# Weights of a seven-product matrix stage prepared three products ahead, with two weight sums in places of their own and one low part on VectorE

## The chip, the cores and the metric

One core of one Trainium2 chip runs the whole program. The metric is the device time of one execution in microseconds (us), the median of several runs. TensorE multiplies, VectorE, ScalarE and GpSimd (POOL) work on tiles in the on-chip memory, and SyncE (SP) issues most of the transfers. Each engine takes its instructions in the order of its own queue and waits on semaphores for the others, so an instruction that waits holds up all behind it on that engine.

## What is computed

One layer of a hybrid decoder trunk in float32: three token mixers (causal pooling, RWKV-7, attention into 256 memory tokens), merged by gates, then a convolutional feed-forward part. The change lies in the feed-forward part, which is, for 1024 tokens of width 1024 and an inner width of 2816:

```python
h = rms_norm(x, norm_ffn_pre[l])
u = causal_dwconv(h @ w_ffn_up[l], conv_w[l], conv_b[l])      # 3 taps along the tokens
u_gate, u_val = jnp.split(u, 2, axis=-1)
f = (jax.nn.gelu(u_gate, approximate=True) * u_val) @ w_ffn_down[l]
x = x + rms_norm(f, norm_ffn_post[l])
```

## The kernel before

**Blocks and pairs.** The inner width is 22 blocks of 128 (NF). A pair i is gate block i and value block 22 + i of `w_ffn_up`. Blocks 0 to 4 are made earlier in another way, in halves of 512 tokens; pairs 5 (EARLY) to 21, 17 in all, run through `up_pair` (L998 to L1079), called by the loop at L1323. The down product `f @ w_ffn_down` follows as passes over 128-wide steps (`down_pass`, `step`).

**Seven products.** The up product of a pair is a 2 × 2 block product: two weight blocks, two halves of the width 1024 (4 slices of 128 each), two halves of the tokens (512 each). It is done with seven products instead of eight, on sums of the quarters. With a11 and a12 the two halves of the gate block, and a21 and a22 those of the value block, the weights of products 0 to 6 are

0: a11; 1: s1 = a21 + a22; 2: s2 = s1 − a11; 3: a12; 4: a11 − a21; 5: a12 − s2; 6: a22.

The token side (panels B11, T1, T2, B21, T3, B22, T4) is made once, ahead of the stage. The results are put together again as they come.

**Float32 out of parts.** Each weight and each panel is kept as a high part, rounded to the matmul's format, and a low part, the rest. `mm3` (L168 to L170) does three matmuls per slice: high × high, high × low, low × high. A product is 4 slices × 3 = 12 matmuls of 128 × 128 by 512 columns, a pair 84, the stage 17 × 84 = 1428.

**What a pair does on each engine.**

- SP loads four weight quarters of two 128 KB pieces each (L1008; `a` in the trace), into places that alternate by the parity of the pair, and stores the result `d_f[i]` (L1079).
- `parts` (L1014): for each of the seven weights ScalarE casts the high part (L1027) and POOL subtracts it from the source for the low part (L1028), in two instructions each, one per 256 columns. The results lie in one of six `wt` places used in turn. So the weights of product m can be written when product m − 6 is through on TensorE.
- `both` (L1010 to L1013): the weight sums, two instructions each. s1 and s2 on POOL, in one tile `sm`, s2 over s1; a11 − a21 over a21 and a12 − s2 over `sm` on VectorE.
- The sums of results: ScalarE copies products 0 and 1 out of PSUM (L1057, L1059), VectorE adds the others (L1061 to L1076; those named `psf` read PSUM).
- The convolution: ScalarE starts it (L1044, 1024 columns, for each block), VectorE adds two taps (L1046, four instructions a pair). ScalarE's gelu (`act`, L200), VectorE's product of gate and value (L1078), the store.

**What sets the order.** `up_pair` writes the steps in the order of the products. A scheduler then orders each engine's queue by what is ready, so parts of the next pair come between those of the pair that is being finished. `last_low` and `last_sum` keep the last POOL low part and the last L1072, behind which the first steps of the down stage are ordered (`later`).

**After the stage.** In the last pair, `down_loads` issues the first three rows of the down product, `X[k]` (rows of `d_f`, L1301), and weights `fw` (L1312), on SP's queue. `step` casts weight and row on ScalarE (L1355) and makes the low parts (L1359) on VectorE or POOL; the results of the down matmuls are `psd`.

The code of the stage, with the line numbers of the profile:

Of the kernel before, what the change touches and what calls it, by code (L numbers as in the profile page):

```python
# [9 lines left out]
F32 = mybir.dt.float32  # L10
FR = mybir.dt.float32r
AF = mybir.ActivationFunctionType
ALU = mybir.AluOpType
# [4 lines left out]
P = 128  # L18
T = 1024
# [9 lines left out]
NF = 22  # L29
# [15 lines left out]
def trunk_kernel(ctx: ExitStack, tc: tile.TileContext, xT, memT, pvec, w_in, w_kv, w_upd, w_upg,  # L45
                 w_pool, w_ppool, w_pmem, w_prwkv, w_o, w_fup, w_fdn, out):
    nc = tc.nc
    V, A, G, PE, SP = nc.vector, nc.scalar, nc.gpsimd, nc.tensor, nc.sync

    const = ctx.enter_context(tc.tile_pool(name="const", bufs=1))  # L50
    wp = ctx.enter_context(tc.tile_pool(name="wp", bufs=1))
    psg = ctx.enter_context(tc.tile_pool(name="psg", bufs=2, space=PSUM))
    psk = ctx.enter_context(tc.tile_pool(name="psk", bufs=1, space=PSUM))
    pss = ctx.enter_context(tc.tile_pool(name="pss", bufs=2, space=PSUM))
# [13 lines left out]
    d_f = dtile([NF, P, T], "d_f")  # L68
# [5 lines left out]
    def col(name, i):  # L74
        o, w = PV[name]
        return pv[:, o + i:o + i + 1]
# [18 lines left out]
    for lo in (0, 64):  # L95
        s = slice(lo, lo + 64)
# [3 lines left out]
    for lo in (0, 64):  # L100
        s = slice(lo, lo + 64)
# [122 lines left out]
    for k in range(KC):  # L224
        tag = ("X01", "X11", "HV", "HV")[k // 2]
# [528 lines left out]
    with tc.tile_pool(name="km", bufs=1) as km:  # L754
# [240 lines left out]

    nwt, last_sum, last_low = [0], [None], [None]

    def up_pair(i):  # L998
        c = i % 2

        def load(nm, tag, j, k0):
            if i == EARLY:
# [3 lines left out]
            t = [wp.tile([P, 2, P], F32, name=nm, tag=f"{tag}{c}", bufs=4) for _ in range(2)]  # L1006
# [4 lines left out]
        def both(eng, out_, a, b, op):  # L1011
            for u in range(2):
                eng.tensor_tensor(out_[u], a[u], b[u], op=op)  # L1013

        def parts(src):

            n = nwt[0] % 6
            nwt[0] += 1
            if n < 2:
                w = ow.tile([P, 2, 4, P], FR, name="wt", tag=f"q{n}")  # L1020
                w = [w[:, 0], w[:, 1]]
            else:
                w = [pmp.tile([P, 4, P], FR, name=f"wt{e}", tag=f"n{8 + (n + 1) % 4 + 4 * e}")
                     for e in range(2)]
            for u in range(2):
                us = slice(2 * u, 2 * u + 2)
                A.copy(w[0][:, us], src[u])  # L1027
                last_low[0] = G.tensor_tensor(w[1][:, us], src[u], w[0][:, us].bitcast(F32), op=ALU.subtract).ins  # L1028
            return w

        nb = [0]

        def prod(src, panel):
            w = parts(src)
            pool, tag = ((psg, "g0"), (psg, "g1"), (pss, "s"), (psk, "k"), (psg, "g0"), (psg, "g1"),
                         (pss, "s"))[nb[0]]
            nb[0] += 1
# [3 lines left out]
            return ps  # L1041

        def convolved(z, d, j):
            A.activation(d, z, AF.Identity, scale=col("cw2", j), bias=col("cb", j))  # L1044
            for n, cw in ((1, "cw1"), (2, "cw0")):
                V.scalar_tensor_tensor(d[:, n:], z[:, :T - n], col(cw, j), d[:, n:], op0=ALU.mult,  # L1046
                                       op1=ALU.add)

        a11 = load("a11", "whi", i, 0)
        a21 = load("a21", "wlo", NF + i, 0)  # L1050
        a22 = load("a22", "wlo", NF + i, 4)
        a12 = load("a12", "whi", i, 4)
        sm = [wp.tile([P, 2, P], F32, name="sm", tag=f"wraw{c}", bufs=3) for _ in range(2)]
        z1, z2 = (ow1.tile([P, T], F32, name=f"z{e}", tag=f"q{4 + 2 * e + c}") for e in range(2))
        c11, c12, c21, c22 = z1[:, :512], z1[:, 512:], z2[:, :512], z2[:, 512:]
        u2 = ow.tile([P, 512], F32, name="u2", tag="xt", bufs=2)
        A.copy(c11, prod(a11, B11))  # L1057
        both(G, sm, a21, a22, ALU.add)
        A.copy(c22, prod(sm, T1))  # L1059
        both(G, sm, sm, a11, ALU.subtract)  # L1060
        V.tensor_tensor(u2, c11, prod(sm, T2), op=ALU.add)  # L1061
        V.tensor_tensor(c22, c22, u2, op=ALU.add)
        V.tensor_tensor(c11, c11, prod(a12, B21), op=ALU.add)
        both(V, a21, a11, a21, ALU.subtract)
        p7 = prod(a21, T3)
        third = V.tensor_tensor(c21, u2, p7, op=ALU.add).ins
        if i == NF - 1:
            down.extend(down_loads())
            down.append(third)
        both(V, sm, a12, sm, ALU.subtract)  # L1070
        V.tensor_tensor(c12, c22, prod(sm, B22), op=ALU.add)
        last_sum[0] = V.tensor_tensor(c22, c22, p7, op=ALU.add).ins  # L1072
        d1, d2 = (ow.tile([P, T], F32, name=f"d{e}", tag=f"q{2 + e}") for e in range(2))
        convolved(z1, d1, i)
        act(d1, d1, AF.Gelu_apprx_tanh)
        V.tensor_tensor(c21, c21, prod(a22, T4), op=ALU.add)  # L1076
        convolved(z2, d2, NF + i)
        V.tensor_tensor(d1, d1, d2, op=ALU.mult)  # L1078
        (G if i == NF - 1 else SP).dma_start(d_f[i], d1)  # L1079


    ow_ctx = ExitStack()
# [82 lines left out]
    EARLY = 5  # L1165
# [109 lines left out]
    class Sums:  # L1275
# [339 lines left out]
```

## Time and profile before

| what | us |
|---|---|
| median of 3 runs | 2079.53 (2077.59 to 2079.88) |
| the profiled execution | 2081.88, its span 2080.0 |
| TensorE busy | 2014.5 |
| VectorE, ScalarE, POOL busy | 1361.4, 1069.4, 812.5 |
| seven-product stage on TensorE | 339.8, from 1499.5 to 1839.3 |

The profiled execution lies 2.35 us above the median, and 1.88 us of it lie outside the span. In the views of the trace a row gives a group of instructions by source line, engine and operation as "output <- inputs"; `wt` are weights in parts, `a` the loaded quarters, `sm` the sums s1 and s2, `z` the results of the pair, `d` the convolved blocks, `psf` the PSUM tiles of the stage. "Idle before" is the time that the engine stood still before the instructions of a group, with what ended it. TensorE's busy time counts each matmul's record, and the record of a matmul that waits runs on, so the number of matmuls per window tells more than its busy share.

### The profile page before, as it was taken

How to read it: one execution, taken by the hardware profiler on the slowest of the kernel's cores; microseconds unless marked ns; L12 is line 12 of the kernel's file. 1: busy time of each engine (PE TensorE's matmuls, PEld its weight loads, DVE VectorE, ACT ScalarE, POOL GpSimd, SP SyncE). 2: the span in 40 equal slices, each digit the busy share in tenths (PEclk: the TensorE clock that was granted, in tenths of full speed). 3: DMA queues.
4: the chain of work that ended last, by engine and by line, in shares of the span. 5: the costliest groups of instructions: out<-in, count | busy, mean ns of one | idle time of the engine just before them, and what ended most of it. 6: DMA issues, size and time to landing. Idle time of an engine off the chain costs nothing.

```text
span 2080.0 us, 34125 instructions
## 1 busy us (share of the span) xinstructions
PE 2014.5 (97%) x12246; PEld 1558.7 (75%) x12246; DVE 1361.4 (65%) x2170; ACT 1069.4 (51%) x2249; POOL 812.5 (39%) x917
## 2 busy tenths in 40 slices
PE   8999999999999999999999999998999999989997
PEld 5777767776778667866878878876678777767886
DVE  6567437664667357823895443778777777767798
ACT  7585348623773367434566243546444443444644
POOL 5521213121222121212133355655588888832341
PEclk9999999999999999999999999999999999999999
DMA  4312211120212021214427343634322222169776
GB/s 155 130 41 74 67 59 61 65 82 22 87 61 98 24 89 61 78 51 133 160 82 234 123 142 110 213 123 135 109 72 76 79 74 83 64 189 261 166 181 149
DMA packets 176713, 221.83 MB, mean 107 GB/s; under 512 B 16544, under 2 KB 128288, under 8 KB 176544
## 3 DMA queue, kind: packets, MB, share of 16 engines
q1 hardware_dynamic: 163616, 204.44, 30.3%
q0 software_dynamic: 11856, 14.16, 4.2%
q8 instruction: 97, 1.59, 0.3%
q10 hardware_dynamic: 1072, 1.05, 0.2%
q14 instruction: 72, 0.59, 0.1%
HBM read 170.30 MB, written 49.28 MB: 106 GB/s over the span
## 4 chain that ended last, share of the span: by engine, by line
PE 30%; DVE 7%; DMA 5%; POOL 4%; issue 4%; ACT 3%; SPq 0%; POOLq 0%; ACTq 0%; DVEq 0%
PE psg L170 5%; PE psg L169 5%; PE psg L168 5%; POOL wt L1028 2%; PE psd L169 2%; PE psd L170 2%; PE psf L170 2%; PE psd L168 2%; PE psf L169 2%; PE psf L168 2%; POOL sm L1013 1%; DMA a<-in_w_fup 1%; DMA g<-d_zg 1%; DMA R<-d_f 1%; POOL wlo L132 1%
## 5 line engine op out<-in xcount | busy, mean ns | idle before, releaser
L132 POOL TENSOR_TENSOR wlo<-wraw,whi 128x256 fp32r<-128x256 f32 x472 | 411.6, 881 | 941.8 <-ACT whi L129 775.1
L168 PE MATMUL psg<-hh,whi 128*128 128x512 f32 x928 | 380.7, 410 | 2.7 <-DVE kv L315 2.7
L170 PE MATMUL psg<-hh,wlo 128*128 128x512 f32 x928 | 376.9, 406 | 0.2
L169 PE MATMUL psg<-hl,whi 128*128 128x512 f32 x928 | 375.8, 405 | 0.0
L129 ACT CAST whi<-wraw 128x256 fp32r<-128x256 f32 x472 | 182.7, 403 | 220.8 <-PE psg L169 108.0
L168 PEld LDWEIGHTS psg<-hh,whi 128*128 128x128 f32 x928 | 174.7, 188 | 43.3 <-DVE kv L315 4.0
L170 PEld LDWEIGHTS psg<-hh,wlo 128*128 128x128 f32 x928 | 174.5, 188 | 43.2 <-POOL wlo L132 5.3
L169 PEld LDWEIGHTS psg<-hl,whi 128*128 128x128 f32 x928 | 174.7, 188 | 39.5 <-issue 3.4
L1028 POOL TENSOR_TENSOR wt<-a,wt 128x256 fp32r<-128x256 f32 x136 | 133.8, 1013 | 31.3 <-ACT wt L1027 31.3
L168 PE MATMUL psd<-f,u 128*128 128x512 f32 x292 | 115.8, 397 | 8.2 <-ACT f L1355 4.8
L169 PE MATMUL psd<-f,u 128*128 128x512 f32 x292 | 115.6, 396 | 0.6 <-DVE f L1359 0.6
L170 PE MATMUL psd<-f,u 128*128 128x512 f32 x292 | 115.2, 396 | 0.0
L1028 POOL TENSOR_TENSOR wt<-sm,wt 128x256 fp32r<-128x256 f32 x102 | 106.8, 1066 | 19.2 <-ACT wt L1027 19.2
L170 PE MATMUL psf<-h2h,wt 128*128 128x512 f32 x272 | 108.8, 400 | 1.0 <-POOL wt L1028 0.6
L168 PE MATMUL psf<-h2h,wt 128*128 128x512 f32 x272 | 106.3, 391 | 1.7 <-ACT wt L1027 1.6
L169 PE MATMUL psf<-h2l,wt 128*128 128x512 f32 x272 | 106.0, 390 | 0.0
L1027 ACT CAST wt<-sm 128x256 fp32r<-128x256 f32 x102 | 37.9, 404 | 129.4 <-POOL sm L1013 124.1
L1046 DVE SCALAR_TENSOR_TENSOR d<-z,pv,d 128x1023 f32<-128x1023 f32 x68 | 91.6, 1347 | 12.0 <-ACT d L1044 9.5
L170 PE MATMUL psf<-t,wt 128*128 128x512 f32 x204 | 80.8, 396 | 3.4 <-POOL wt L1028 3.4
L686 DVE TENSOR_TENSOR HV<-ph,Hd 64x128 f32<-64x128 f32 x112 | 32.4, 289 | 72.2 <-PE ph L640 48.0
L168 PE MATMUL psf<-t,wt 128*128 128x512 f32 x204 | 79.6, 390 | 0.0
L169 PE MATMUL psf<-t,wt 128*128 128x512 f32 x204 | 79.5, 390 | 0.0
(424 smaller groups left out, 4750.7 us busy)
## 6 DMA issues: line engine op xcount, KB each, us to landing
wraw<-in_w_in SPq DMA_DIRECT2D x240, 128.0 KB, 2.4
a<-in_w_fup SPq DMA_DIRECT2D x128, 128.0 KB, 2.4
d_zg<-st SPq DMA_DIRECT2D x48, 256.0 KB, 2.7
wraw<-in_w_fup SPq DMA_DIRECT2D x80, 128.0 KB, 2.5
fw<-in_w_fdn SPq DMA_DIRECT2D x33, 256.0 KB, 4.2
fraw<-d_f SPq DMA_DIRECT2D x33, 256.0 KB, 5.3
wraw<-in_w_prwkv SPq DMA_DIRECT2D x64, 128.0 KB, 2.4
wraw<-in_w_o SPq DMA_DIRECT2D x64, 128.0 KB, 2.5
```

Of the source, the lines that this page charges most:

```text
L129: last_whi[0] = A.copy(hi, src).ins
L132: (V if lo_on_dve[0] else G).tensor_tensor(lo, src, hi.bitcast(F32), op=ALU.subtract)
L168: first = PE.matmul(ps, wh, xh, start=start, stop=False)
L169: PE.matmul(ps, wh, xl, start=False, stop=False)
L170: last_mm[0] = PE.matmul(ps, wl, xh, start=False, stop=stop).ins
L686: ready = V.tensor_tensor(HV[q, :, c + 1, e], ph[q], Hd[q], op=ALU.add).ins
L1013: eng.tensor_tensor(out_[u], a[u], b[u], op=op)
L1027: A.copy(w[0][:, us], src[u])
L1028: last_low[0] = G.tensor_tensor(w[1][:, us], src[u], w[0][:, us].bitcast(F32), op=ALU.subtract).ins
L1046: V.scalar_tensor_tensor(d[:, n:], z[:, :T - n], col(cw, j), d[:, n:], op0=ALU.mult, op1=ALU.add)
```

## The change

`up_pair` becomes a class `Pair` with a method for each part and a loop `up_pairs` that writes the steps in another order:

- **Three products ahead (AHEAD).** The weights of product m (cast, low part, the sums made for it) are written ahead of the matmuls and result sums of product m − 3. The six places of `wt` stay.
- **Loads and the first two sums one pair ahead.** `sums` issues a pair's four loads and makes s1 and s2 at the place where the pair before gets its weights of product 4. s1 has the places that `sm` had, s2 a place of its own (tag `ss`). Only in pair 5 s2 is still written over s1.
- **One low part on VectorE.** The low part of product 1 (weights s1) is made by VectorE instead of POOL: two instructions a pair, 34 in all.
- **Two orders.** s1 stands behind the last POOL low part written so far (`last_low`), a11 − a21 behind the last L1103 (`last_sum`).

What is computed, the matmuls and their order, and the order of the loads and stores on SP are the same.

```diff
-    def up_pair(i):
-        c = i % 2
+    def parts(src, eng):
...
-                last_low[0] = G.tensor_tensor(w[1][:, us], src[u], w[0][:, us].bitcast(F32), op=ALU.subtract).ins
+            low = eng.tensor_tensor(w[1][:, us], src[u], w[0][:, us].bitcast(F32), op=ALU.subtract)
+            if eng is G:
+                last_low[0] = low.ins
...
+    class Pair:
...
+        def weights(self, n):
+            if n == 2 and self.s2 is self.s1:
+                both(G, self.s2, self.s1, self.a11, ALU.subtract)
+            if n == 4:
+                both(V, self.a21, self.a11, self.a21, ALU.subtract, last_sum[0])
+            if n == 5:
+                both(V, self.s2, self.a12, self.s2, ALU.subtract)
+            src = (self.a11, self.s1, self.s2, self.a12, self.a21, self.s2, self.a22)[n]
+            return parts(src, V if n == 1 else G)
+
+        def sums(self):
+            self.a11 = self.load("a11", "whi", self.i, 0)
...
+            self.s1 = [wp.tile([P, 2, P], F32, name="s1", tag=f"wraw{self.c}", bufs=3) for _ in range(2)]
+            both(G, self.s1, self.a21, self.a22, ALU.add, last_low[0])
+            if self.i == EARLY:
+                self.s2 = self.s1
             else:
+                t = ow.tile([P, 4, P], F32, name="s2", tag="ss", bufs=2)
+                self.s2 = [t[:, :2], t[:, 2:]]
+                both(G, self.s2, self.s1, self.a11, ALU.subtract)
...
+    AHEAD = 3
+
+    def up_pairs(i0, i1):
+        pairs = [Pair(i) for i in range(i0, i1)]
+        pairs[0].sums()
+        steps = [(p, n) for p in pairs for n in range(7)]
+        ready = []
+        for m in range(len(steps) + AHEAD):
+            if m < len(steps):
+                p, n = steps[m]
+                if n == 4 and p is not pairs[-1]:
+                    pairs[p.i - i0 + 1].sums()
+                ready.append(p.weights(n))
+            if m >= AHEAD:
+                p, n = steps[m - AHEAD]
+                p.product(n, ready.pop(0))
...
-    for i in range(EARLY, NF):
-        up_pair(i)
+    up_pairs(EARLY, NF)
```

In the changed kernel the low part is L1011, the sums of weights L1018, the cast L1010, the convolution L1023 and L1025, the copies L1082 and L1085, the sums of results L1088 to L1110, the product L1112, the store L1113.

Three queues show the new order. In the rows below, a name's number is that of its tile; a pair's loads are four numbers apart each (first piece and second piece one apart), and from one pair to the next the numbers grow by some 180.

POOL before, in the middle of the stage. The weights are those of one pair, from product 0 (a_16302) to product 3 (a_16314), and a_16485 + a_16489 is s1 of the pair after it:

```order
L1028 TENSOR_TENSOR wt<-a_16302,wt 128x256
L1028 TENSOR_TENSOR wt<-a_16303,wt 128x256
L1013 TENSOR_TENSOR sm<-a_16485,a_16489 128x256
L1013 TENSOR_TENSOR sm<-a_16486,a_16490 128x256
L1028 TENSOR_TENSOR wt<-sm,wt 128x256 x2
L1013 TENSOR_TENSOR sm<-sm,a_16302 128x256
L1013 TENSOR_TENSOR sm<-sm,a_16303 128x256
L1028 TENSOR_TENSOR wt_16366<-sm,wt_16365 128x256 x2
L1028 TENSOR_TENSOR wt_16387<-a_16314,wt_16386 128x256
L1028 TENSOR_TENSOR wt_16387<-a_16315,wt_16386 128x256
```

The second sum (`sm<-sm,a_16302`) stands behind the low part of product 1 and ahead of that of product 2. POOL in the changed kernel, again from product 0 of a pair (a_16188) on:

```order
L1011 TENSOR_TENSOR wt<-a_16188,wt 128x256
L1011 TENSOR_TENSOR wt<-a_16189,wt 128x256
L1011 TENSOR_TENSOR wt_16322<-s_16208,wt_16321 128x256 x2
L1011 TENSOR_TENSOR wt_16347<-a_16200,wt_16346 128x256
L1011 TENSOR_TENSOR wt_16347<-a_16201,wt_16346 128x256
L1018 TENSOR_TENSOR s_16385<-a_16373,a_16377 128x256
L1018 TENSOR_TENSOR s_16386<-a_16374,a_16378 128x256
L1018 TENSOR_TENSOR s_16389<-s_16385,a_16369 128x256
L1018 TENSOR_TENSOR s_16389<-s_16386,a_16370 128x256
L1011 TENSOR_TENSOR wt_16395<-a_16192,wt_16394 128x256
L1011 TENSOR_TENSOR wt_16395<-a_16193,wt_16394 128x256
```

The low part of product 1 is gone from POOL, and both sums of the next pair (s_16385 and s_16389) stand behind the low part of product 3, ahead of that of product 4.

VectorE before, through the sums of results of one pair (z_17756, z_17757). a_17930 is a12 of the next pair, a_18102 a21 of the one after that:

```order
L1013 TENSOR_TENSOR a_18102<-a_18098,a_18102 128x256
L1013 TENSOR_TENSOR a_18103<-a_18099,a_18103 128x256
L1061 TENSOR_TENSOR u_17758<-z_17756,psf 128x512
L1062 TENSOR_TENSOR z_17757<-z_17757,u_17758 128x512
L1063 TENSOR_TENSOR z_17756<-z_17756,psf 128x512
L1013 TENSOR_TENSOR sm<-a_17930,sm 128x256
L1013 TENSOR_TENSOR sm<-a_17931,sm 128x256
L1066 TENSOR_TENSOR z_17757<-u_17758,psf 128x512
L1071 TENSOR_TENSOR z_17756<-z_17757,psf 128x512
L1072 TENSOR_TENSOR z_17757<-z_17757,psf 128x512
L1046 SCALAR_TENSOR_TENSOR d_17887<-z_17756,pv,d_17887 128x1023
L1076 TENSOR_TENSOR z_17757<-z_17757,psf 128x512
```

VectorE in the changed kernel, through the same sums of one pair (z_17630, z_17631); the s and a rows are weights of the next pair:

```order
L1088 TENSOR_TENSOR u_17632<-z_17630,psf 128x512
L1011 TENSOR_TENSOR wt_17741<-s_17650,wt_17740 128x256
L1089 TENSOR_TENSOR z_17631<-z_17631,u_17632 128x512
L1011 TENSOR_TENSOR wt_17741<-s_17651,wt_17740 128x256
L1092 TENSOR_TENSOR z_17630<-z_17630,psf 128x512
L1018 TENSOR_TENSOR s_17654<-a_17646,s_17654 128x256
L1018 TENSOR_TENSOR s_17654<-a_17647,s_17654 128x256
L1096 TENSOR_TENSOR z_17631<-u_17632,psf 128x512
L1102 TENSOR_TENSOR z_17630<-z_17631,psf 128x512
L1103 TENSOR_TENSOR z_17631<-z_17631,psf 128x512
L1018 TENSOR_TENSOR a_17638<-a_17634,a_17638 128x256
L1018 TENSOR_TENSOR a_17639<-a_17635,a_17639 128x256
```

The low part of product 1 (L1011) has come in around L1089, a12 − s2 is now ahead of the fourth result sum as before, and a11 − a21 stands behind L1103.

ScalarE before, from the casts of product 0 of a pair (a_16481) to the gelu of the pair ahead of it (d_16451):

```order
L1027 CAST wt<-a_16481 128x256
L1027 CAST wt<-a_16482 128x256
L1027 CAST wt_16523<-sm 128x256 x2
L1027 CAST wt_16545<-sm 128x256 x2
L1027 CAST wt_16566<-a_16493 128x256
L1027 CAST wt_16566<-a_16494 128x256
L1027 CAST wt_16588<-a_16485 128x256
L1027 CAST wt_16588<-a_16486 128x256
L1044 ACTIVATE d_16451<-z_16320,pv 128x1024
L1027 CAST wt<-sm 128x256 x2
L1044 ACTIVATE d_16452<-z_16321,pv 128x1024
L200 ACTIVATE d_16451<-d_16451 128x1024
```

ScalarE in the changed kernel, from the casts of product 0 of a pair (a_16550) on:

```order
L1010 CAST wt_16636<-a_16550 128x256
L1085 COPY z_16547<-psf 128x512
L1010 CAST wt_16636<-a_16551 128x256
L1010 CAST wt_16656<-s_16566 128x256
L1010 CAST wt_16656<-s_16567 128x256
L1010 CAST wt_16683<-s_16570 128x256 x2
L1010 CAST wt_16708<-a_16562 128x256
L1010 CAST wt_16708<-a_16563 128x256
L1023 ACTIVATE d_16677<-z_16546,pv 128x1024
L1010 CAST wt<-a_16554 128x256
L1010 CAST wt<-a_16555 128x256
L1010 CAST wt<-s_16570 128x256 x2
```

The casts of product 4 (a_16485 before, a_16554 now) stood ahead of the start of the convolution of the pair that is being finished and now stand behind it.

More of the change, by code (lines that the diff above doesn't have):

```diff
@@ L996, in trunk_kernel, with both, convolved, __init__ @@
     nwt, last_sum, last_low = [0], [None], [None]
-    def up_pair(i):
-        c = i % 2
-        def load(nm, tag, j, k0):
-            if i == EARLY:
+    def parts(src, eng):
+        n = nwt[0] % 6
+        nwt[0] += 1
+        if n < 2:
+            w = ow.tile([P, 2, 4, P], FR, name="wt", tag=f"q{n}")
+            w = [w[:, 0], w[:, 1]]
+        else:
+            w = [pmp.tile([P, 4, P], FR, name=f"wt{e}", tag=f"n{8 + (n + 1) % 4 + 4 * e}")
+                 for e in range(2)]
+        for u in range(2):
+            us = slice(2 * u, 2 * u + 2)
+            A.copy(w[0][:, us], src[u])
+            low = eng.tensor_tensor(w[1][:, us], src[u], w[0][:, us].bitcast(F32), op=ALU.subtract)
+            if eng is G:
+                last_low[0] = low.ins
+        return w
+    def both(eng, out_, a, b, op, behind=None):
+        for u in range(2):
+            i = eng.tensor_tensor(out_[u], a[u], b[u], op=op)
+            if behind is not None:
+                later(i, behind)
+    def convolved(z, d, j):
+        A.activation(d, z, AF.Identity, scale=col("cw2", j), bias=col("cb", j))
+        for n, cw in ((1, "cw1"), (2, "cw0")):
+            V.scalar_tensor_tensor(d[:, n:], z[:, :T - n], col(cw, j), d[:, n:], op0=ALU.mult,
+                                   op1=ALU.add)
+    class Pair:
+        def __init__(self, i):
+            self.i, self.c = i, i % 2
+        def load(self, nm, tag, j, k0):
+            if self.i == EARLY:
                 t = ow.tile([P, 4, P], F32, name=nm, tag="xt" if tag == "whi" else "ss", bufs=2)
@@ L1051, in up_pair @@
[L1051 to L1079, printed above, removed]
+            getattr(self, f"sum{n}")(ps)
@@ new lines, in sum0, with sum1, sum2 @@
+        def sum0(self, ps):
+            z = [ow1.tile([P, T], F32, name=f"z{e}", tag=f"q{4 + 2 * e + self.c}") for e in range(2)]
+            self.z = z
+            self.c11, self.c12, self.c21, self.c22 = z[0][:, :512], z[0][:, 512:], z[1][:, :512], z[1][:, 512:]
+            self.u2 = ow.tile([P, 512], F32, name="u2", tag="xt", bufs=2)
+            A.copy(self.c11, ps)
+        def sum1(self, ps):
+            A.copy(self.c22, ps)
+        def sum2(self, ps):
+            V.tensor_tensor(self.u2, self.c11, ps, op=ALU.add)
+            V.tensor_tensor(self.c22, self.c22, self.u2, op=ALU.add)
@@ new lines, in sum3, with sum4, sum5 @@
+        def sum3(self, ps):
+            V.tensor_tensor(self.c11, self.c11, ps, op=ALU.add)
+        def sum4(self, ps):
+            self.p7 = ps
+            third = V.tensor_tensor(self.c21, self.u2, ps, op=ALU.add).ins
+            if self.i == NF - 1:
+                down.extend(down_loads())
+                down.append(third)
+        def sum5(self, ps):
+            V.tensor_tensor(self.c12, self.c22, ps, op=ALU.add)
+            last_sum[0] = V.tensor_tensor(self.c22, self.c22, self.p7, op=ALU.add).ins
+            self.d = [ow.tile([P, T], F32, name=f"d{e}", tag=f"q{2 + e}") for e in range(2)]
+            convolved(self.z[0], self.d[0], self.i)
+            act(self.d[0], self.d[0], AF.Gelu_apprx_tanh)
```

43 lines of the change are left out of this document (14 added, 29 removed).

## The prediction

> **What bounds the kernel now.** The page first: TensorE is busy almost throughout, so the question is what it loses inside the stage that is changed.
>
> ```profile
> span 2080.0 us, 34125 instructions
> PE 2014.5 (97%) x12246; PEld 1558.7 (75%) x12246; DVE 1361.4 (65%) x2170; ACT 1069.4 (51%) x2249; POOL 812.5 (39%) x917
> ```
>
> Second, the busy times by window. After the window and its length, each row has PE, PEld, DVE, ACT and POOL with counts, then the granted clock, the DMA share and GB/s; the last row is the whole stage.
>
> ```profile
> 1562.00:1582.00 20.00, 20.00 (x90) 16.57 (x89) 14.74 (x17) 8.99 (x19) 17.24 (x19) 1.00 0.24 78
> 1602.00:1622.00 20.00, 19.97 (x88) 15.84 (x87) 14.73 (x17) 9.00 (x19) 17.25 (x19) 1.00 0.25 80
> 1662.00:1682.00 20.00, 19.60 (x85) 15.31 (x84) 14.77 (x17) 8.91 (x19) 17.25 (x19) 1.00 0.23 80
> 1782.00:1802.00 20.00, 19.57 (x84) 15.34 (x83) 14.79 (x17) 8.99 (x19) 17.29 (x19) 1.00 0.23 79
> 1499.50:1839.30 339.80, 333.75 (x1429) 264.73 (x1428) 252.09 (x274) 151.68 (x321) 284.87 (x295) 1.00 0.23 75
> ```
>
> 90 matmuls in 20 us before about 1610, 84 or 85 after it, at the same full clock: TensorE turns from dense to slightly starved. A "busy" of 19.6 hides this, since a waiting matmul's record overlaps the next. Third, TensorE's timeline in the dense part, first and last of 98 matmuls:
>
> ```profile
> 1559.95 0.39 PE L168 MATMUL psf<-h2h,wt 128*128 128x512 f32 x1
> 1581.94 0.39 PE L169 MATMUL psf<-t,wt 128*128 128x512 f32 x1
> ```
>
> 21.99 us over 97 steps is 0.2267 us a matmul when fed. A pair has 84, so 19.04 us; the 1428 of the stage need 323.7, and it lasts 339.8, so 16.1 us are lost. Fourth, ScalarE's timeline of one instruction per pair (the copy of product 0), three of 16:
>
> ```profile
> 1530.73 0.57 ACT L1057 COPY z<-psf 128x512 f32<-128x512 f32 x1
> 1611.62 0.57 ACT L1057 COPY z<-psf 128x512 f32<-128x512 f32 x1
> 1833.97 0.57 ACT L1057 COPY z<-psf 128x512 f32<-128x512 f32 x1
> ```
>
> (1833.97 − 1530.73)/15 is 20.22 us, and it is the same 20.22 from 1530 to 1611, while TensorE was dense. So something else turns at 20.2 us a pair, TensorE at 19.04 uses up its lead by about 1610, and then follows. The waits of the stage say what:
>
> ```profile
> ACT wt L1027 <- POOL sm L1013: 118.8, 32, 7.1
> DVE a L1013 <- POOL sm L1013: 53.9, 29, 3.9
> POOL wt L1028 <- ACT wt L1027: 49.5, 34, 8.7
> ACT d L1044 <- DVE z L1071: 36.1, 16, 4.4
> PEld psf L170 <- POOL wt L1028: 18.5, 39, 1.0
> DVE sm L1013 <- POOL wt L1028: 15.2, 16, 3.5
> ACT wt L1027 <- DMA d_f<-ug: 10.2, 2, 5.3
> ```
>
> No engine is full (POOL, the fullest, 17.25 of 20). It is a ring of in-order queues: POOL's sums let ScalarE cast and VectorE form a11−a21; POOL's low parts free `sm` for VectorE's a12−sm; behind this stand the sums of products 4 and 5, which ScalarE's convolution start awaits; behind that stand the casts of the next weights, which POOL awaits. TensorE's stall is the end of it (`psf <- POOL wt`).
>
> **The change, part by part.** Durations of the stage, by line:
>
> ```profile
> L1028 POOL TENSOR_TENSOR wt<-a,wt 128x256 fp32r<-128x256 f32 x132 | 129.9, 1013 | 31.3 <-ACT wt L1027 31.3
> L1046 DVE SCALAR_TENSOR_TENSOR d<-z,pv,d 128x1023 f32<-128x1023 f32 x64 | 86.5, 1351 | 12.0 <-ACT d L1044 9.5
> L1028 POOL TENSOR_TENSOR wt<-sm,wt 128x256 fp32r<-128x256 f32 x98 | 103.5, 1075 | 18.2 <-ACT wt L1027 18.2
> L1013 DVE TENSOR_TENSOR sm<-a,sm 128x256 f32<-128x256 f32 x32 | 31.4, 1021 | 15.2 <-POOL wt L1028 15.2
> L1013 POOL TENSOR_TENSOR sm<-sm,a 128x256 f32<-128x256 f32 x32 | 29.7, 947 | 0.0
> L1078 DVE TENSOR_TENSOR d<-d,d 128x1024 f32<-128x1024 f32 x16 | 25.2, 1576 | 1.7
> L1013 POOL TENSOR_TENSOR sm<-a,a 128x256 f32<-128x256 f32 x32 | 24.0, 752 | 9.6 <-DMA a<-in_w_fup 7.9 <-POOL sm L1013 1.7
> L1062 DVE TENSOR_TENSOR z<-z,u 128x512 f32<-128x512 f32 x17 | 20.0, 1176 | 1.8
> ```
>
> *POOL.* Two of 14 low parts a pair leave it: about 2 × 1.04 us. Its load goes from 17.25 × 20.22/20 = 17.4 to about 15.4 us a pair, against TensorE's 19.04. The four sums stay (3.4 us). Today the second is written over the first, so it must follow the low part of product 1, and the cast of product 2 must follow it; with places of their own both are made before that pair's casts begin. The waits of 118.8 and 53.9 us on POOL's sums go.
>
> *VectorE.* The two low parts come to it. It has no low part of 256 columns in this stage today; its subtractions of that size, with both operands in SBUF, bound the price:
>
> ```profile
> 1658.26 0.43 DVE L1013 TENSOR_TENSOR a<-a,a 128x256 f32<-128x256 f32 x1 [2.71 <-POOL sm L1013]
> 1659.64 0.94 DVE L1013 TENSOR_TENSOR a<-a,a 128x256 f32<-128x256 f32 x1 [0.95 <-POOL sm L1013]
> 1657.50 0.73 POOL L1013 TENSOR_TENSOR sm<-a,a 128x256 f32<-128x256 f32 x1
> 1668.42 3.33 POOL L1028 TENSOR_TENSOR wt<-sm,wt 128x256 fp32r<-128x256 f32 x2 [0.85 <-ACT wt L1027]
> ```
>
> 0.43 us with POOL idle, 0.94 with POOL at work, and 1.02 in the mean of a12−sm. VectorE is nearly always beside POOL here, so I take 1.02: 2.0 us a pair (0.9 at the other end). Its load goes from 14.77 × 1.011 = 14.9 to 17.0 a pair. It becomes the fullest engine behind TensorE, with 2.0 us to spare. If the a11−a21 that run at 0.43 today were all slowed to 0.94, it would be half a microsecond more.
>
> *ScalarE.* The same instructions, some 9 us a pair; only its order changes.
>
> *The ring.* A weight's place is free again when the product six earlier is through. Cast and low part then take 2 × 0.40 and 2 × 1.04 us, and 5 × 2.72 = 13.6 us are left until the product starts. Followed by the order of the changed kernel, with E3 the end of product 3: the low parts of product 2 are done at about E3 + 2.5, a12−s2 at E3 + 4.2, the sum of product 4 just behind that, the sums of product 5 at E5 + 1.2, a11−a21 at E5 + 3.1, each in time for a cast whose place comes free at E5 or E6. So every queue waits for TensorE, and low parts are ready some 9 us before use. What is late next is VectorE, by the 2 us above. Then the pair takes 19.04. The loss ran from about 1611 to 1839.3, 228 us or 11.3 periods: 11.3 × (20.22 − 19.04) = **13.3 us**. Of the 16.1 the rest is the start of the stage (casts behind a store, `ACT wt <- DMA d_f<-ug`), which the change leaves.
>
> *Loads.* Four weight loads a pair stand in the same order on SP's queue; they wait for places, the a22 load by some 4 us in hand. Price nothing; if late, the sum a21+a22 waits in POOL as it does today (7.9 us in the stage).
>
> *The end of the stage.* Today VectorE and ScalarE lag TensorE by some 12 us, and the down stage pays:
>
> ```profile
> 1837.60 0.32 SPq L1079 DMA_DIRECT2D d_f<-d  x1
> 1838.01 1.74 SPq L1301 DMA_DIRECT2D X<-d_f  x3
> 1842.91 1.96 ACT L1355 CAST f<-X 128x512 fp32r<-128x512 f32 x3 [5.72 <-DMA X<-d_f]
> 1839.04 0.40 PE L170 MATMUL psf<-h2h,wt 128*128 128x512 f32 x1
> 1843.58 0.80 PE L168 MATMUL psd<-f,u 128*128 128x512 f32 x1 [4.14 <-ACT f L1355]
> 1843.50:1849.50 6.00, 5.92 (x14) 4.42 (x15) 5.91 (x8) 3.88 (x6) 1.29 (x1) 0.52 1.08 364
> 1865.00:1869.20 4.20, 0.80 (x5) 0.34 (x4) 0.13 (x1) 0.73 (x2) 0.00 (x0) 1.00 1.08 335
> 1869.20:1875.00 5.80, 5.80 (x18) 4.37 (x19) 2.34 (x4) 2.19 (x5) 1.28 (x1) 0.71 1.09 357
> ```
>
> The X loads stand on SP's queue behind the store of pair 20, which waits for L1078. TensorE idles 4.3 us (1839.27 to 1843.58) and then runs at a granted 0.52, 14 matmuls in 6.0 us: 6.0 − 14 × 0.2267 = 2.8 more. With the lag gone, that store is ready some 8 us before the stage ends and X lands, at 4.9 us from issue (1838.01 to 1842.91), before it. So up to 7.1 come back. The second stop, 1865 to 1869, waits for a weight load while the DMA engines are at 1.08, and moves along with the stage; with X and others moved ahead of the stage's end it may shrink too (up to 3.4 and 5.8 − 18 × 0.2267 = 1.7), or, if the transfers are the limit, take back what the first gives. Bounds 0 and 12.2; I take **6.5**, near the 7.1 of the rows.
>
> Sum: 13.3 + 6.5 = 19.8 us off 2081.88, the profiled execution's time (1.88 outside its span), so 2062.1. That execution is 2.35 above the median 2079.53; off the median it is 2059.7, rounded to **2060**. About 0.2% (4 us) is what a measurement here tells from no change.
>
> **The rivals.** *VectorE and POOL in each other's way.* The rows under VectorE show it: 0.43 turns into 0.94, and POOL's 0.73 into 1.66 beside the convolution. If such operations exclude one another, moving a low part from one to the other frees little. At durations alone: POOL 18 × 0.73 = 13.1 a pair now, 16 × 0.73 = 11.7 then; VectorE's with both operands in SBUF 4 × 0.43 now, 6 × 0.43 then, and 4 × 1.35 + 1.58 + 1.18 = 8.2 in both (recorded, so too high). 23.0 now, 22.5 then. Today's pair takes 20.2, so the count is at least 2.8 too high, and the pair to come is at most 19.7 if this were the limit. That gives 11.3 × 0.5 = 5.7, with 6.5 at the end 12: 2067; with nothing at the end 2074. The Trainium skill's page SBUF — State Buffer (section "SBUF: two separate sides") states such a rule: VectorE operations with two SBUF inputs and GpSimd operations that read SBUF hold one port pair for the whole instruction, and the other blocks. Taken literally the rule would give 22.5 us a pair and some 38 us more, and the trace, with 20.2 for a counted 23.0, does not bear it out to that extent. For: VectorE is nearly always beside POOL. Against: the ring explains 20.2 without it. Chance 0.17.
>
> *Slower.* VectorE now stands in order at the low part of product 1 (waits for ScalarE) and at a12−s2 (waits for POOL's low part of product 2); behind it wait sums of products 3 to 5, behind these ScalarE's convolution start, behind that the casts, behind those POOL. The ring closes again if these waits use up the 9 us in hand. From 20.2 us a pair on it is a loss over all 16.5 pairs: at 20.8, 0.6 × 16.5 = 10 us, 2089. For: the 15.2 us that VectorE waits at this place today. Against: the sums that opened that wait are made a pair ahead. Chance 0.06.
>
> *No change in substance.* TensorE is starved by something that stays (places of weights, loads): 2078. The dense stretch before 1610 speaks against it. Chance 0.05.
>
> **How the numbers follow.** The forecast has 0.72. Its own range is 2054 (13.3 + 12.2) to 2066 (13.3 + 0); the first rival reaches to 2074, of which I take in 2072. Faster by over 0.2%: 0.72 and nearly all of 0.17; slower 0.06; the same 0.07.
>
> **What would show it.** Right: 88 to 90 matmuls per 20 us through the whole stage; the copy of product 0 every 19.0 us; VectorE near 17.9 of 20 and POOL near 16; no `ACT wt <- POOL` sums in the waits; granted clock near 1.00 at the start of the down stage. Wrong: 84 to 86 matmuls again with VectorE above 18 and TensorE waiting for a low part (first rival), or POOL and ScalarE waiting for VectorE's rows (second), or an idle as long as today's at the first `psd`.

## The result and the profile after

The changed kernel takes 2057.53 us in the median (2054.62 to 2061.56, 4 runs) against 2079.5 before: a ratio of 0.9892, 95% interval 0.9877 to 0.9907, or 22.0 us less. The forecast was 2060, 19.5 less. The profiled execution took 2058.67 (span 2056.8), 23.2 less than the one before. Its parts, from the first and last matmuls of each stage:

| part | before | after | gained | forecast |
|---|---|---|---|---|
| before the stage | 1499.7 | 1498.9 | 0.8 | – |
| the stage, 1428 matmuls | 339.5 | 325.0 | 14.5 | 13.3 |
| from its end to the last down matmul | 214.9 | 207.0 | 7.9 | 6.5 |

The busy times by window in the changed kernel (PE, PEld, DVE, ACT, POOL, clock, DMA share, GB/s):

```profile
1562.00:1582.00 20.00, 20.00 (x90) 16.58 (x89) 18.48 (x20) 10.54 (x21) 19.67 (x19) 1.00 0.27 88
1662.00:1682.00 20.00, 20.00 (x89) 16.55 (x89) 17.04 (x20) 9.19 (x19) 17.52 (x18) 1.00 0.26 84
1742.00:1762.00 20.00, 20.00 (x90) 16.56 (x89) 16.42 (x20) 9.96 (x21) 16.90 (x17) 1.00 0.25 80
1498.70:1823.90 325.20, 324.18 (x1431) 268.20 (x1429) 274.52 (x312) 158.06 (x325) 278.98 (x264) 1.00 0.25 83
```

89 or 90 matmuls in every 20 us, where before it was 84 or 85 in most of the stage. The stage lasts 325.0 us for matmuls that need 323.7. VectorE and POOL are busier per window: the pair is shorter, VectorE has two more instructions a pair, POOL's low parts take longer (below), and in the first row both still catch up. ScalarE's copy of product 0, which came every 20.22 us, shows this: four pairs from 1527.04 to 1599.56, 18.13 us a pair, and about 19.0 us a pair after that. The waits of the stage:

```profile
ACT d L1023 <- DVE z L1102: 51.9, 17, 6.4
POOL wt L1011 <- ACT wt L1010: 36.7, 29, 6.8
ACT wt L1010 <- PE psf L169: 33.5, 27, 2.0
ACT wt L1010 <- POOL wt L1011: 28.2, 14, 2.5
DVE z L1102 <- PE psf L170: 26.3, 14, 2.0
ACT wt L1010 <- PE psf L170: 14.6, 8, 2.2
```

The two waits on POOL's sums (118.8 and 53.9 us) are gone. In their place ScalarE's casts and VectorE's sums wait for `PE psf`: the other engines now follow TensorE. The durations of the operations that were moved, or that lie beside them:

```profile
L1011 POOL TENSOR_TENSOR wt<-a,wt 128x256 fp32r<-128x256 f32 x132 | 152.9, 1182 | 35.6 <-ACT wt L1010 35.6
L1025 DVE SCALAR_TENSOR_TENSOR d<-z,pv,d 128x1023 f32<-128x1023 f32 x66 | 98.6, 1497 | 2.1
L1011 DVE TENSOR_TENSOR wt<-s,wt 128x256 fp32r<-128x256 f32 x32 | 23.2, 725 | 3.2 <-ACT wt L1010 3.2
L1018 DVE TENSOR_TENSOR s<-a,s 128x256 f32<-128x256 f32 x32 | 22.1, 729 | 2.8 <-POOL wt L1011 2.3
```

A low part on VectorE costs 0.73 us, not 1.02; POOL's went from 1.01 to 1.18 and the convolution from 1.35 to 1.50. At the end of the stage (SP's queue, TensorE):

```profile
1812.48 0.32 SPq L1113 DMA_DIRECT2D d_f<-d  x1
1815.93 1.27 SPq L1352 DMA_DIRECT2D X<-d_f  x3
1823.67 0.39 PE L170 MATMUL psf<-h2h,wt 128*128 128x512 f32 x1
1823.90 0.39 PE L168 MATMUL psd<-f,u 128*128 128x512 f32 x1
1848.20 0.50 PE L168 MATMUL psd<-f,u 128*128 128x512 f32 x1 [2.38 <-ACT u L1405]
1848.20:1853.20 5.00, 5.00 (x14) 3.72 (x15) 2.77 (x5) 2.34 (x4) 1.28 (x1) 0.66 1.09 353
```

The X loads go out 8 us before the stage ends, and the first down matmul follows without a gap, with a granted clock of 1.00 in the 5 us behind it. The stop for a weight load, 3.4 us before, is 2.4.

### The profile page after: what moved, and what is told of

Its sections match the earlier page's. It is cut to its first block, busy times and chain, and to the rows that moved or that the text cites. A ratio compares the mean times of both kernels' runs of the same rounds, so it can differ in the third digit from the quotient of the medians.

```text
span 2056.8 us, 34070 instructions
## 1 busy us (share of the span) xinstructions
PE 2000.2 (97%) x12246; PEld 1558.2 (76%) x12246; DVE 1378.4 (67%) x2204; ACT 1073.6 (52%) x2249; POOL 804.4 (39%) x883
## 5 line engine op out<-in xcount | busy, mean ns | idle before, releaser
L1011 POOL TENSOR_TENSOR wt<-a,wt 128x256 fp32r<-128x256 f32 x136 | 156.7, 1176 | 35.6 <-ACT wt L1010 35.6
L1025 DVE SCALAR_TENSOR_TENSOR d<-z,pv,d 128x1023 f32<-128x1023 f32 x68 | 101.1, 1491 | 2.2
L1011 POOL TENSOR_TENSOR wt<-s,wt 128x256 fp32r<-128x256 f32 x68 | 80.3, 1201 | 3.4 <-ACT wt L1010 2.1
L1023 ACT ACTIVATE d<-z,pv 128x1024 f32<-128x1024 f32 x34 | 42.4, 1246 | 67.6 <-DVE z L1102 51.9
```

The lines of the kernel that those rows point to most:

```text
L1011: low = eng.tensor_tensor(w[1][:, us], src[u], w[0][:, us].bitcast(F32), op=ALU.subtract)
```

## The experiments

Theory after the result: the ring is open, that is, the other engines no longer hold one another at 20.22 us a pair, and TensorE sets the pair. Open was which part of the change opens it, and whether the 7.9 us at the end are the idle and the half clock that the prediction counted. Ratios are against the kernel before, run each time on the same chip as the version (medians 2076.9 to 2077.1); "stage" is the time on TensorE in the profiled execution from the first matmul of the stage to its last.

### The changed kernel once more

> The changed kernel itself, as a measure for the others on the same chip. Expected from its first measurement: 0.989 of the kernel before.

0.9907 (0.9890 to 0.9925), 2056.75 us, stage 325.2. The other ratios are to be held against this one.

### The parts of the change taken back one at a time

Low part of product 1 back on POOL:

```diff
-            return parts(src, V if n == 1 else G)
+            return parts(src, G)
```

> The changed kernel with the low part of product 1 back on POOL; all else as changed. Ring theory (the order and the places of the sums opened the ring; the engine of one low part matters little): VectorE falls to some 15 us a pair, POOL rises to 14 low parts and four sums. At the durations of the kernel before that is 17.4 us a pair, under TensorE's 19.04: 2057 to 2060. Rival, POOL's load was the point (at the changed kernel's durations, 14 x 1.18 + 2 x 0.78 + 2 x 0.75 = 19.6 us a pair, over 19.04): TensorE would lose 0.6 us a pair once its lead of some 9 us is used up, so up to 5 us at the end of the stage and the lag at the down stage back, 2060 to 2068.

0.9917 (0.9900 to 0.9935), 2058.82 us; stage 325.8. The ring is open without VectorE's low part. POOL is then full for most of the stage: 20.00 of 20.

```profile
1602.00:1622.00 20.00, 20.00 (x90) 16.57 (x89) 17.59 (x17) 10.15 (x23) 20.00 (x20) 1.00 0.25 80
```

ScalarE's copies of product 0 show what a full POOL means:

```profile
1526.49 0.57 ACT L1082 COPY z<-psf 128x512 f32<-128x512 f32 x1
1712.99 0.57 ACT L1082 COPY z<-psf 128x512 f32<-128x512 f32 x1
```

Ten pairs in 186.5 us, 18.65 us a pair, still a little less than TensorE's 19.04. So the rival's 19.6 was too high. The margin is 0.4 us, where the changed kernel, at 18.13, has 0.9: this version holds with little to spare.

s2 over s1 in every pair:

```diff
-            if self.i == EARLY:
+            if True:
                 self.s2 = self.s1
```

> The changed kernel with s2 written over s1 in every pair, as in pair 5: made by POOL when product 2's weights are made, behind the low part of product 1. Ring theory in its wide form (weights three products ahead leave some 9 us in hand, of which this edge takes about 3): 2057 to 2060. Rival, the place of its own for s2 is what opened the ring: a period between 19.5 and 20.2 us, 2062 to 2078, with waits of ScalarE's cast for POOL's sum back near 100 us.

0.9908 (0.9893 to 0.9923), 2057.35 us, stage 323.7. A place of its own for s2 is not what opened the ring either. ScalarE's wait for POOL's sums is back, but at 37.8 us from 1600 to 1800 (77.5 in the kernel before), and TensorE runs dense beside it.

No lead:

```diff
-    AHEAD = 3
+    AHEAD = 0
```

> The changed kernel with AHEAD 0: weights written right ahead of their product's matmuls; the orders, the places and VectorE's low part stay. The queues come out nearly as in the changed kernel, so by the run of the loop alone it should make no difference: ratio 0.989 to 0.992. If the lead is needed after all: 0.994 or more.

0.9899 (0.9879 to 0.9918), 2057.26 us, stage 324.7. Writing the weights three products ahead changes nothing that can be measured: from 1560 to 1780 us the instructions of ScalarE, VectorE and POOL come in the same order as in the changed kernel, so the scheduler made the same queues of both ways of writing.

### Parts of the change alone

The low part of product 1 on VectorE, in the kernel before:

```diff
-        def parts(src):
+        def parts(src, eng=G):
...
-            w = parts(src)
+            w = parts(src, V if nb[0] == 1 else G)
```

> The kernel before with the low part of product 1 on VectorE, nothing else changed. Ring theory: the period of 20.2 us is made of waits in turn, not of POOL's load; the low parts of product 1 only change their engine within the ring, so 20.0 to 20.6 us a pair, 2075 to 2086. Rival, load theory: 2 us less on POOL a pair take 1 us or more off the period, 2060 to 2068.

1.0018 (1.0009 to 1.0027), 2080.06 us, stage 343.2. Two microseconds less work a pair on POOL gain nothing: the limit was not POOL's load.

The new loop alone:

```diff
-            return parts(src, V if n == 1 else G)
+            return parts(src, G)
...
-            if self.i == EARLY:
+            if True:
...
-                both(V, self.a21, self.a11, self.a21, ALU.subtract, last_sum[0])
+                both(V, self.a21, self.a11, self.a21, ALU.subtract)
...
-            both(G, self.s1, self.a21, self.a22, ALU.add, last_low[0])
+            both(G, self.s1, self.a21, self.a22, ALU.add)
...
-                if n == 4 and p is not pairs[-1]:
-                    pairs[p.i - i0 + 1].sums()
+                if n == 0:
+                    p.sums()
```

> The changed kernel's new loop (weights written three products ahead) alone: the low part of product 1 on POOL, s2 written over s1, loads and s1 made where the pair's own weights begin, and neither of the two orders (a11-a21 behind the last L1103, s1 behind the last POOL low part). Theory L, that writing the weights three products ahead gives the 9 us in hand: near the changed kernel, 2055 to 2062. Theory P, that the places of a11-a21 on VectorE and of s1 on POOL closed the ring (the scheduler puts them early, where they wait for the a21 and a22 loads of a pair to come, and those loads for places that the low part of product 6 frees), and that the loop by itself leaves the queues as they were: 2073 to 2082, copies of product 0 every 20.2 us.

0.9996 (0.9986 to 1.0006), 2075.06 us, stage 337.1. The copies of product 0, second and sixteenth of 17:

```profile
1529.86 0.57 ACT L1082 COPY z<-psf 128x512 f32<-128x512 f32 x1
1812.91 0.57 ACT L1082 COPY z<-psf 128x512 f32<-128x512 f32 x1
```

283.05/14 is 20.22 us, the old period to the hundredth, and from 1560 to 1780 us the three queues stand in the order of the kernel before. So the loop gains nothing without the rest, and by the run at AHEAD 0 the lead adds nothing to the rest. The loads and sums one pair ahead are in neither of the two tests; the run with both orders, below, speaks of them.

### The two orders

Only a11 − a21 behind the last sum of product 5 (L1072), in the kernel before:

```diff
-        both(V, a21, a11, a21, ALU.subtract)
+        both(V, a21, a11, a21, ALU.subtract, last_sum[0])
```

> The kernel before with one order added: a11-a21 stands behind the last L1072 on VectorE, as in the changed kernel. Theory P: this takes VectorE's wait for s1 (53.9 us in the stage) off the sums of results, which opens the ring: the stage dense, 2055 to 2064. Theory L: no change, 2075 to 2082. Between (2065 to 2074) if s1's place on POOL closes it again by ScalarE's casts.

1.0109 (1.0089 to 1.0128), 2099.73 us, stage 360.3: the opposite of what theory P expected. The copies come every 21.7 us in the mean (20.7 to 23.4). Part of a pair on POOL, then what waits for it on VectorE and ScalarE:

```profile
1709.80 0.74 POOL L1013 TENSOR_TENSOR sm<-a,a 128x256 f32<-128x256 f32 x1 [1.72 <-PE psf L169]
...
1711.86 0.74 POOL L1013 TENSOR_TENSOR sm<-a,a 128x256 f32<-128x256 f32 x1
1712.56 1.43 POOL L1030 TENSOR_TENSOR wt<-sm,wt 128x256 fp32r<-128x256 f32 x2
1713.95 1.43 POOL L1013 TENSOR_TENSOR sm<-sm,a 128x256 f32<-128x256 f32 x2
1715.34 1.43 POOL L1030 TENSOR_TENSOR wt<-sm,wt 128x256 fp32r<-128x256 f32 x2
...
1716.11 1.83 DVE L1013 TENSOR_TENSOR sm<-a,sm 128x256 f32<-128x256 f32 x2 [6.89 <-POOL wt L1030]
...
1714.72 0.41 ACT L1029 CAST wt<-sm 128x256 fp32r<-128x256 f32 x1 [9.14 <-POOL sm L1013]
```

s1 of the next pair (1709.80) still stands on POOL ahead of this pair's products 1 and 2, and stops POOL until it can be made (in nine other pairs from 1600 to 1800 it waits for the load of a quarter, 13.0 us in all); behind it wait s2 (1713.95), the low part of product 2, VectorE's a12 − s2 for 6.89 us and ScalarE's cast for 9.14. VectorE no longer waits for s1 at a11 − a21, but a11 − a21, and all that follows from it, comes later.

Only s1 behind the low part of product 3, in the kernel before (`low3` is the last low part when product 3 of the pair ahead is written):

```diff
-        both(G, sm, a21, a22, ALU.add)
+        both(G, sm, a21, a22, ALU.add, low3[0])
```

> The kernel before with the other order added: s1 of the next pair stands on POOL behind the low part of product 3 of the pair, as in the changed kernel. By then its loads have landed, so POOL does not wait for them and VectorE's a11-a21 does not wait long for s1. Theory P: the ring opens here too, 2055 to 2064. Theory L: no change, 2075 to 2082. If only VectorE's order matters, and not POOL's: 2075 to 2082 here and a gain in the run before this one.

1.0048 (1.0033 to 1.0064), 2086.14 us, stage 344.0, a copy every 20.6 us. Slower too. VectorE's wait for s1 falls from 35.0 to 7.3 us from 1600 to 1800, but a12 − s2 waits 35.1 us for POOL's low parts, where it waited 7.3. Which edge gives just 20.6 wasn't followed further.

Both orders in the kernel before: the two edits above together.

> The kernel before with both orders of the changed kernel: a11-a21 behind the last L1072 on VectorE, and s1 behind the low part of product 3 on POOL; s2 still over s1, all low parts on POOL, no new loop. If the two orders together are what opens the ring (alone each cost time, since the one makes the other's wait longer): the stage dense, 0.989 to 0.994 of the kernel before, 2054 to 2065. If besides the orders VectorE's low part or the place for s2 is needed, which two runs have taken away one at a time: VectorE's a12-s2 still stands behind POOL's low parts of products 1 and 2 with s2 between them, a period of 20 us or more, ratio 0.998 to 1.010.

0.9938 (0.9920 to 0.9956), 2064.16 us, with ten runs from 2057.6 to 2077.0, far wider apart than any other version's. The profiled execution is the slowest of them:

```profile
1562.00:1582.00 20.00, 20.00 (x90) 16.57 (x89) 14.50 (x16) 8.89 (x19) 19.12 (x20) 1.00 0.27 93
1662.00:1682.00 20.00, 20.00 (x90) 16.55 (x89) 15.40 (x19) 8.90 (x19) 19.12 (x20) 1.00 0.23 80
1782.00:1802.00 20.00, 19.97 (x87) 15.72 (x86) 15.39 (x17) 8.91 (x19) 19.12 (x20) 1.00 0.23 80
```

Dense for most of the stage, and copies every 19.1 us (1554.26 to 1688.07, seven pairs), then 21 to 22 us for some pairs toward the end; in the first of these POOL waits 3.5 us for a cast, 0.9 in the pairs of 19.1. Why was not followed. The stage takes 333.1. Each order alone costs time; both together gain 13 us of the 20. What they leave is a period of 19.1 at best, just over TensorE's 19.04, with no margin. The low part on VectorE or the place for s2, either of them (the first two runs), goes with a margin. The rest of the loop, loads and sums one pair ahead, is the rival here, since those two runs have it too. The traces speak against it: from 1560 to 1780 us ScalarE's order is the same in this run, in both of those and in the changed kernel, and POOL and VectorE differ from it by the place of s2 alone in the first, by the engine of the low part alone in the second.

### More on VectorE

```diff
-            return parts(src, V if n == 1 else G)
+            return parts(src, V if n in (1, 3, 5) else G)
```

> The changed kernel with the low parts of products 1, 3 and 5 on VectorE instead of that of product 1 alone: four more instructions a pair there. At 0.73 us to 0.95 us each VectorE goes from 16.4 us (17.2 of 20) to 19.3 to 20.2 us a pair, over TensorE's 19.04, and POOL to some 13. By the load: 0.3 to 1.1 us a pair lost, less the lead, so 0 to 15 us more than the changed kernel, ratio 0.991 to 0.998. If the two engines only hold one port in turn, the sum of their work is unchanged or less: ratio 0.989 to 0.991.

0.9896 (0.9880 to 0.9912), 2056.76 us, stage 323.7, the matmuls' own time.

```profile
1562.00:1582.00 20.00, 20.00 (x90) 16.57 (x89) 19.86 (x24) 9.09 (x21) 14.83 (x14) 1.00 0.26 87
1662.00:1682.00 20.00, 20.00 (x90) 16.58 (x89) 18.60 (x24) 9.27 (x19) 13.03 (x14) 1.00 0.24 80
1742.00:1762.00 20.00, 20.00 (x90) 16.58 (x89) 17.69 (x23) 9.29 (x19) 13.59 (x13) 1.00 0.26 88
```

Four more instructions a pair leave VectorE at 17.7 of 20 once it has caught up, 1.3 more than with one low part there (16.4 at the same place), and not the 3 that the load account counted; POOL falls to 13.6. The load account fails: with POOL less busy, VectorE's other instructions run faster, L1089 at 0.79 us instead of 1.22, a11 − a21 at 0.42 instead of 0.63. The two engines' busy time together falls from 33.3 (16.42 + 16.90) to 31.3 of 20 us each. That is the direction of the second account, in which they take turns at something they share, and its ratio was met; but nothing here was held up by it, so its limit stays unseen.

### The end of the stage

The first row X issued late, about as in the kernel before: one VectorE copy of one column into its place, behind the sums of product 5 of the last pair.

```diff
+            if self.i == NF - 1:
+                down[:0] = down_loads(self.c22)
...
         X = panel_slots("X", "h2h0", 0)
+        V.tensor_copy(X[0][:, :1], gate[:, :1])
```

> The changed kernel with one more VectorE copy of one column, behind the two sums of product 5 of the last pair, into the place of the first row X of the down product: X is issued some 1.3 us before the stage ends, as in the kernel before, instead of some 8 us. The stage itself stays. If the end of the stage was worth what the prediction counted (an idle of 4.3 us, then 2.8 us at half clock): 7 us more, 2064 to 2066. If the down stage evens it out (transfers at their limit in any case): within 2 us of 2057.5.

0.9915 (0.9900 to 0.9930), 2059.02 us. In the trace the stage takes 324.7, and from its end to the last down matmul 207.4, against 207.0 in the changed kernel. The 0.4 us tell nothing: in the five other traces that leave this end as in the changed kernel the part takes 206.6 to 208.1. Only the first row is late (1821.12, 0.4 us before the stage ends); the other two still go out at 1813.57, while in the kernel before all three went out 1.3 us before the end. Yet an idle is there. TensorE's timeline and the window behind it:

```profile
1824.79 1.19 PE L168 MATMUL psd<-f,u 128*128 128x512 f32 x4 [3.10 <-ACT f L1407]
...
1824.70:1829.70 5.00, 4.35 (x12) 3.16 (x12) 4.89 (x6) 3.53 (x5) 0.36 (x1) 0.66 0.96 308
```

3.1 us of idle, then a clock of 0.66, and the later stop for a weight load is gone in return. Here an idle at the start only moves the stop; it is not time that is lost on top.

ScalarE's casts late, as in the kernel before: twelve copies behind the last gelu, and the casts of steps 3 to 5 behind these.

```diff
+            if self.i == NF - 1:
+                for _ in range(12):
+                    c = A.copy(self.u2, self.c22)
+                    later(c, phase[1][-1])
+                    busy[0] = c.ins
...
+            if 3 <= n < 6:
+                later(hi, busy[0])
```

> The changed kernel with twelve copies of 512 columns on ScalarE behind the gelu of the last pair, and the casts of steps 3 to 5 of the down stage behind them: some 6 us, so that the cast of step 3 comes some 12 us after the end of the stage, as in the kernel before; the rows X come early as in the changed kernel. Theory C: what the end of the stage gained is the time at which ScalarE's casts free the places of the next weight loads, since the transfers limit the first 30 us of the down stage and stood idle for some 7 us before: 4 to 7 us more than the changed kernel, ratio 0.993 to 0.995. The prediction's account (only the idle ahead of the first down matmul and the half clock after it): within 1 us, ratio 0.990 to 0.991.

0.9914 (0.9890 to 0.9938), 2060.26 us: the interval reaches from no difference to the changed kernel to what theory C wanted, so the median does not decide. In the trace the cast of step 3 comes 12.6 us after the stage (before 12.4, in the changed kernel 5.0), as it was meant to, and the end takes 209.6 us instead of 207.0, 2.6 more, with a stop of 5.4 us for the late casts and the later one gone. Of the 7.9 us, then, the first row late alone gives nothing that can be told, and the casts alone some 2.6. What they give together, with all three rows and the late VectorE, was not tried.

## Why the prediction was right

**What bounds.** As put: TensorE needs 19.04 us a pair, the ring turned at 20.22, and with the ring open TensorE sets the pace. The gain in the stage was 14.5 where 13.3 were forecast; the 1.2 more lies at the stage's start, which was to stay as it was and lost 1.3 instead of some 2.5. That start differs among the runs with an open ring too: their stages take 323.7 to 325.8, the matmuls' own time being 323.7.

**What the engines carry.** POOL was put at 15.4 us a pair and takes 278.98/325.2 × 19.04 = 16.3; VectorE was put at 17.0 and takes 16.1. The low parts on VectorE cost 1.45 a pair, not 2.0: the price was taken from a12 − s2, which runs at 0.73 itself in the new order, not at 1.02. POOL pays part of it back with slower low parts, 1.18 for 1.01, so that POOL, and not VectorE, is the fullest behind TensorE.

**The step that was wrong.** The prediction had the waits on POOL's sums go because s2 has a place of its own and is made ahead. The runs show that this place isn't needed (0.9908), nor the low part on VectorE (0.9917), nor the three products' lead (0.9899). What opens the ring in these runs are the two orders, which the walk used ("a11−a21 at E5 + 3.1") without naming them as the cause: together 0.9938, each alone 1.0109 and 1.0048. The low part or the place for s2 then only adds the margin. Whether both of these without the orders, or the place for s2 alone, would do it too was not run; the low part alone does not (1.0018). The number could not show this: the forecast of the stage priced the change as a whole, an open ring against a closed one, and so came out right whichever part opens it.

**The end of the stage.** 6.5 was forecast and 7.9 came. TensorE's stops account for it. Before, the first cost 7.1 us with its low clock, the second 3.4 + 1.7; in the changed kernel the first is gone and the second costs 2.4 + 1.8, so 8.0 less. But the step that gave the first stop a price of its own (7.1, "come back") does not hold: with one row late it is there again, 3.1 us and another 2.2 behind it (12 matmuls in 4.9 us, 4.9 − 12 × 0.2267), and the end is no longer than without it, since the later stop is gone. With the casts late there is one stop too, of 5.4 us and 1.8 behind it. The kernel before pays for two, and why it does stays open. It is also at the upper end: the four versions whose ring stays closed, with the same end, take 212.7 to 213.5 us there, not 214.9. So that the forecast for this part came near is partly luck. A candidate is the transfers. Of the kernel before, SP's queue and the DMA share:

```profile
1846.20 0.37 SPq L1312 DMA_DIRECT2D fw<-in_w_fdn  x1
1854.81 0.37 SPq L1312 DMA_DIRECT2D fw<-in_w_fdn  x1
1849.30:1859.30 10.00, 10.00 (x46) 8.27 (x45) 8.45 (x11) 6.14 (x10) 2.15 (x2) 1.00 0.75 258
```

and of the changed kernel, the same two loads, and the window at the same distance from the end of the stage (10 to 20 us):

```profile
1827.62 0.59 SPq L1363 DMA_DIRECT2D fw<-in_w_fdn  x1
1832.04 0.37 SPq L1363 DMA_DIRECT2D fw<-in_w_fdn  x1
1833.90:1843.90 10.00, 10.00 (x46) 8.29 (x45) 4.84 (x7) 4.35 (x7) 1.33 (x1) 1.00 1.11 295
```

The third and fourth weight loads after the stage stood 8.6 us apart and now 4.4, and the DMA engines, whose share is above 1.0 in most of the next 30 us of both kernels, work at 1.11 instead of 0.75. That the late loads, behind ScalarE's casts of a pair that lagged by 12 us, are what cost the time is argued from the queue and not shown: with the casts late these two loads stand 10.2 us apart (1831.29 and 1841.50), further than before, and the end is longer by 2.6, not by 7.9.

**The rivals.** VectorE and POOL do slow each other, as the rows show, but not to 19.7 us a pair: POOL full to the last tenth turned at 18.65, and three low parts on VectorE cost nothing. The Trainium skill's rule (SBUF — State Buffer, "SBUF: two separate sides"), counted literally in the prediction's estimate, asked for 22.5 us a pair; the trace has 19.04. The slower case, a ring slower than the old one, happened clearly only in the runs with one order.

## What to carry to other kernels

When a stage runs at a steady period that no engine's load explains, look for an instruction that a scheduler has put early in an in-order queue and that waits there for a load. Move such instructions in all the queues of the ring at once: each move alone made this kernel slower, by 0.5 and 1.1%, and both together faster. And an idle behind a stage may cost nothing by itself: before counting it as gain, see whether a later stop takes its place when it goes or comes.

## What the runs showed of the hardware

The length of a stop of TensorE does not tell by itself whether the granted clock falls behind it. In the 5 us behind the stop the clock was 1.00 after 1.60 us (at 1515.26 in the kernel before) and after 3.00 us (at 1873.34 with only s1 behind), but 0.71 after 1.55 us (at 1883.98 with three low parts on VectorE), 0.66 after 2.38 us in the changed kernel, and 0.50 after 4.14 us:

```profile
1873.34 0.50 PE L168 MATMUL psd<-f,u 128*128 128x512 f32 x1 [3.00 <-ACT u L1358]
1873.30:1878.30 5.00, 4.96 (x21) 3.80 (x22) 2.84 (x5) 2.47 (x4) 1.26 (x1) 1.00 1.09 357
1883.98 0.49 PE L168 MATMUL psd<-f,u 128*128 128x512 f32 x1 [1.55 <-ACT f L1405]
1883.90:1888.90 5.00, 4.68 (x13) 3.54 (x14) 4.87 (x8) 3.63 (x8) 0.00 (x0) 0.71 1.15 243
```

What decides was not followed. In the changed kernel the drop cost 1.8 us: 14 matmuls in 5 us, 5 − 14 × 0.2267, with the clock at 0.50 from 1848.57 to 1851.98.

The same subtraction of 256 columns on VectorE took 0.43 us with POOL idle and 0.94 with POOL at work in the kernel before; a11 − a21 took 0.41 to 1.00 in the changed kernel, and 0.42 in the mean from 1530 to 1800 with three low parts on VectorE. The sums with one operand in PSUM took 0.67 to 0.69 us in all three traces from 1530 to 1800, with POOL idle or at work. A price taken from one order does not hold in another.
